# Five own buffers for the modulation columns in the SwiGLU stages, and a new division of the columns over the stages

## The chip, the cores and the metric

The kernel runs on one core of a Trainium2 chip. The metric is the time of one execution on the device in microseconds, as the median of several runs. The engines of a core work side by side, each through its own instructions in order: TensorE (PE; its weight loads stand apart as PEld), VectorE (DVE), ScalarE (ACT), GpSimd (POOL) and SyncE (SP), which here issues all loads.

## The reference, cut to what matters

A stream `x` of 256 tokens by 1024 channels goes through four layers. Each layer is a half-weighted SwiGLU part, a token mixer (RWKV-7, Mamba-2, sliding-window attention, RWKV-7) and a second SwiGLU part. Everything is float32. Ahead of each part the stream is normed and modulated by shift, scale and gate, which come from one vector `c`:

```python
c_act = jax.nn.silu(c)
...
    mod = (c_act @ ada_w[i] + ada_b[i]).reshape(bsz, N_SUB, 3, d)
    shift, scale, gate = mod[:, :, 0], mod[:, :, 1], mod[:, :, 2]
    h = adaln(x, norm_g[i, 0], shift[:, 0], scale[:, 0])
    x = x + MACARON_W * gate[:, 0, None] * swiglu(h, ffn_w_in[i, 0], ffn_w_out[i, 0])
...
def swiglu(h, w_in, w_out):
    a, b = jnp.split(h @ w_in, 2, axis=-1)
    return (jax.nn.silu(a) * b) @ w_out
```

`ada_w` has 1024 x 9216 numbers for each of the four layers, so 9 x 8 = 72 columns of 128 results, 288 in all. They depend on `c` alone: each can be computed at any time before the part that uses it.

## The kernel before

The stream stays in SBUF as `x`, eight tiles of 128 channels by 256 tokens. The stages follow each other: for layer i, `ffn{i}0`, the mixer, `ffn{i}2`, so eight SwiGLU stages (the text names them `ffn00` to `ffn32`, layer first) and four mixers: rw0 (RWKV), the Mamba stage, the attention stage and rw1 (the second RWKV stage, in layer 3).

**Units.** Weights come in units of 128 x 1024 numbers (512 KB). `unit` loads one into a `raw` buffer (four of them, pool `wp`), ScalarE copies it rounded to `whi` (L299), VectorE subtracts to get the rest, `wlo` (L303), and TensorE multiplies three times (L328 to L330, or L520 to L522 in the output projection): high by high, high by low, low by high. In a SwiGLU stage there are 66 units, 24 matmuls each: 44 into the two halves of the hidden part, 22 out of it. `weights` sets how many pairs `whi`, `wlo` are there: seven in a SwiGLU stage. The hidden tiles pass through `done` in `ffn` (L675 to L679). The output projection (`out_proj`) keeps sums of all eight tiles in PSUM and holds its last units back; when they come, each tile is summed into x (L608), and the next stage's operands are made of it at once (L491, L605).

**Columns.** One modulation column is one load of 512 KB and one operation on VectorE that multiplies, sums and adds the bias (L253; a readout of the sum belongs to it), and for scale and gate one more small operation (L257, L261). `mod_step` does both, and takes its buffer from the same four `raw` as the weights. `todo` is the list of columns in the order of use. In SwiGLU and Mamba stages `mod_tick` is called once in each unit and issues a column whenever its credit has grown to one; `mod_plan` sets how many a stage does (`QUOTA`) and over how many units. In the RWKV stages `mod_some` issues them at places in the code, up to the count `ahead`. Whatever is then still missing, `mod_until` issues right before it is used, which is in `out_proj`, ahead of the sums into x.

**Order.** A scheduler places the instructions on each engine's queue from the program and its dependencies. SP's queue is in order: a load that waits for its buffer holds up the loads behind it. `hold` and `issue_after` forbid some instructions to stand ahead of a given one.

## Time and profile before

| | |
|---|---|
| median of 3 runs | 2522.41 us (2514.05 to 2526.98) |
| profiled execution | 2529.85 us, its span 2527.9 us |
| columns in the twelve stages, in their order | 40, 36, 28, 28, 7, 28, 28, 13, 24, 24, 32, 0 |
| mean granted clock of TensorE | 0.962 of full speed |

Rows of groups give the line, the engine, the operation, its tiles as out<-in, the count, the busy time, the mean of one in ns, and the idle time of the engine ahead of them with what ended most of it. Rows that begin with two times are a stretch of the span and its length, the busy time of each engine with its instructions, the clock, the share of the DMA engines and their rate. Rows of waits name who waited, for whom, how long in all, how often and the longest. Rows of the timeline begin with the start and the duration in us.

### The profile page before, as it was taken

The page shows a single profiled execution, that of the slowest core. Times are in us where ns is not written, and L with a number is a line of the kernel's source. Part 1 is how long each engine was busy: PE and PEld are TensorE (multiplying, and loading weights), DVE is VectorE, ACT ScalarE, POOL GpSimd, SP SyncE. Part 2 cuts the span into 40 slices and gives each one's busy share as a digit, 9 for nine tenths or more (in the row PEclk, how much of TensorE's full clock was granted, in tenths as well). Part 3 has the DMA queues.
Part 4 walks back from the last instruction along what each step waited for, and adds up shares of the span by engine and source line. Part 5 has one row for each costly group of instructions (what it writes and reads, how often), then busy time and mean ns, then how long its engine had stood idle before and what let it go on. Part 6 is the DMA issues. An engine that isn't in the chain of part 4 may idle for free.

```text
span 2527.9 us, 51852 instructions
## 1 busy us (share of the span) xinstructions
PE 2403.7 (95%) x20868; PEld 2247.2 (89%) x20868; DVE 1984.8 (79%) x4181; ACT 1262.2 (50%) x2261; POOL 8.1 (0%) x14
## 2 busy tenths in 40 slices
PE   6999999989999989999999999899999999998999
PEld 5998877789999988999999999799999977777999
DVE  7777687887788788988878878987788767867754
ACT  3445663254454466765445446554444465623543
POOL 0000000000000000000000000000000000000000
PEclk9999898699999999999999999989999999987999
DMA  8874224668858834455885884468758732255653
GB/s 304 288 262 167 92 94 158 234 202 291 274 196 287 285 128 135 152 178 198 302 282 188 294 286 166 151 213 293 257 180 299 263 119 72 81 174 195 211 189 117
DMA packets 145392, 521.98 MB, mean 206 GB/s; under 512 B 16128, under 2 KB 19456, under 8 KB 145024
## 3 DMA queue, kind: packets, MB, share of 16 engines
q1 hardware_dynamic: 145152, 518.67, 60.3%
q8 instruction: 164, 2.69, 0.4%
q14 instruction: 76, 0.62, 0.1%
HBM read 516.50 MB, written 2.10 MB: 205 GB/s over the span
## 4 chain that ended last, share of the span: by engine, by line
PE 52%; DMA 20%; DVE 18%; ACT 5%; issue 5%; DVEq 0%; ACTq 0%; SPq 0%
DMA raw<-ffn 11%; PE aux L1077 8%; DMA ada<-ada_w 7%; DVE wlo L303 7%; PE aux L330 5%; PE aux L328 5%; PE aux L329 5%; PE mm L328 5%; PE mm L329 4%; PE mm L330 4%; PE mm L521 3%; DVE ada L253 3%; PE mm L520 3%; PE mm L522 3%; ACT whi L299 3%
## 5 line engine op out<-in xcount | busy, mean ns | idle before, releaser
L299 ACT CAST whi<-raw 128x1024 fp32r<-128x1024 f32 x671 | 699.9, 1049 | 696.1 <-DMA raw<-ffn 476.6
L303 DVE TENSOR_TENSOR wlo<-raw,whi 128x1024 fp32r<-128x1024 f32 x671 | 816.0, 1221 | 244.0 <-ACT whi L299 240.8
L328 PE MATMUL aux<-hh,whi 128*128 128x256 f32 x2576 | 723.7, 281 | 18.6 <-DVE ft L676 16.0
L330 PE MATMUL aux<-hh,wlo 128*128 128x256 f32 x2576 | 722.1, 281 | 12.7 <-DVE wlo L303 12.4
L329 PE MATMUL aux<-hl,whi 128*128 128x256 f32 x2576 | 720.3, 280 | 0.0
L328 PEld LDWEIGHTS aux<-hh,whi 128*128 128x128 f32 x2576 | 487.7, 189 | 24.7 <-DVE ft L676 20.1
L330 PEld LDWEIGHTS aux<-hh,wlo 128*128 128x128 f32 x2576 | 488.0, 190 | 16.1 <-DVE wlo L303 16.1
L329 PEld LDWEIGHTS aux<-hl,whi 128*128 128x128 f32 x2576 | 488.2, 190 | 0.0
L253 DVE CUSTOM_DVE_ANT_0 ada<-ada,cb,vec 128x1024 f32<-128x1024 f32 x288 | 368.3, 1280 | 82.9 <-DMA ada<-ada_w 82.2
L520 PE MATMUL mm<-gh,whi 128*128 128x256 f32 x1408 | 393.4, 281 | 9.9 <-ACT gh L678 9.9
L522 PE MATMUL mm<-gh,wlo 128*128 128x256 f32 x1408 | 391.7, 281 | 3.6 <-DVE wlo L303 3.5
L521 PE MATMUL mm<-gl,whi 128*128 128x256 f32 x1408 | 393.5, 281 | 0.8 <-DVE gl L679 0.5
L328 PE MATMUL mm<-hh,whi 128*128 128x256 f32 (+1 forms) x1056 | 311.3, 301 | 13.5 <-ACT cy L885 5.1
L329 PE MATMUL mm<-hl,whi 128*128 128x256 f32 (+1 forms) x1056 | 306.3, 293 | 0.4
L330 PE MATMUL mm<-hh,wlo 128*128 128x256 f32 (+1 forms) x1056 | 305.6, 292 | 0.0
L520 PEld LDWEIGHTS mm<-gh,whi 128*128 128x128 f32 x1408 | 266.9, 190 | 11.5 <-ACT gh L678 11.5
L522 PEld LDWEIGHTS mm<-gh,wlo 128*128 128x128 f32 x1408 | 266.2, 190 | 4.9 <-DVE wlo L303 4.8
L521 PEld LDWEIGHTS mm<-gl,whi 128*128 128x128 f32 x1408 | 267.0, 190 | 2.4 <-DVE gl L679 2.4
L328 PEld LDWEIGHTS mm<-hh,whi 128*128 128x128 f32 x1056 | 203.2, 195 | 27.7 <-issue 6.8
L329 PEld LDWEIGHTS mm<-hl,whi 128*128 128x128 f32 x1056 | 205.8, 195 | 8.7 <-issue 2.3
L330 PEld LDWEIGHTS mm<-hh,wlo 128*128 128x128 f32 x1056 | 205.3, 195 | 5.9 <-issue 4.3
L678 ACT ACTIVATE gh<-ft 128x256 fp32r<-128x256 f32 x176 | 73.0, 416 | 142.2 <-DVE ft L677 141.4
(357 smaller groups left out, 2998.7 us busy)
## 6 DMA issues: line engine op xcount, KB each, us to landing
raw<-ffn SPq DMA_DIRECT2D x522, 512.0 KB, 4.6
ada<-ada_w SPq DMA_DIRECT2D x288, 512.0 KB, 4.4
raw<-rkv SPq DMA_DIRECT2D x48, 512.0 KB, 3.3
raw<-mbin SPq DMA_DIRECT2D x48, 512.0 KB, 3.3
raw<-rwo SPq DMA_DIRECT2D x16, 512.0 KB, 4.6
raw<-mbout SPq DMA_DIRECT2D x16, 512.0 KB, 3.2
lora<-lora SPq DMA_DIRECT2D x12, 512.0 KB, 3.3
raw<-qkv SPq DMA_DIRECT2D x12, 512.0 KB, 4.0
```

Of the source, the lines that this page charges most:

```text
L253: nc.vector.tensor_tensor_reduce(out=raw, in0=raw, in1=self.cb, scale=1.0, scalar=self.v("ada_b", i * 72 + col), op0=ALU.mult, op1=ALU.add ...
L299: nc.scalar.copy(hi[:, :n], raw[:, :n])
L303: nc.vector.tensor_tensor(lo[:, :n], raw[:, :n], hi[:, :n].bitcast(F32), ALU.subtract)
L328: mm(out, hi, xh, start=start, stop=False)
L329: mm(out, hi, xl, start=False, stop=False)
L330: mm(out, lo, xh, start=False, stop=stop)
L520: mm(o, hi, xh, start=k == 0 and j % 2 == 0, stop=False, skip_group_check=True)
L521: mm(o, hi, xl, start=False, stop=False, skip_group_check=True)
L522: mm(o, lo, xh, start=False, stop=k == n - 1 and j % 2 == 1, skip_group_check=True)
L678: nc.scalar.activation(gh, t, AF.Copy, scale=0.5)
L1077: ins = nc.tensor.matmul(*a, **k)
```

## The change

In the SwiGLU stages the columns get a pool of their own, `ap`, of five buffers, and the pairs of prepared weights go from seven to six. A column is now fetched (`mod_fetch`) some time before it is computed: up to five are in hand (two in the first stage), one fetch in each unit. The computing begins ten units into the stage (in the first one at once) and is spread over 50 units instead of 52.8. The computation stands no longer in the scope of `hold`, but is bound to come after the subtraction of its unit (`part`). What is in hand at the end of a stage's hidden units is computed there.

The columns of the twelve stages become 40, 24, 33, 33, 6, 34, 34, 4, 32, 32, 8, 8. The attention stage has no rate of its own in either kernel: what it computes is what `mod_until` finds missing there. In rw0 four of the 24 are such, while none was before.

```diff
@@ -22,7 +22,7 @@
 S = 256
 DEPTH = 4
 
-QUOTA = ((24, 28), (28, 28), (28, 24), (24, 0))
+QUOTA = ((24, 33), (33, 34), (34, 32), (32, 8))
 DFF = 2816
 NJ = D // P
 NF = DFF // P
@@ -231,6 +231,7 @@
                     self.todo += [(i, s, 1, j), (i, s, 0, j)]
                 self.todo += [(i, s, 2, j) for j in range(NJ)]
         self.todo.reverse()
+        self.coming, self.apool, self.lead = [], None, 0
         self.credit = self.rate = 0.0
         self.st = None
         self.ready = []
@@ -244,12 +245,18 @@
         at, _ = V_AT[name]
         return self.vec[:, at + j : at + j + n]
 
+    def mod_fetch(self, pool, tag):
+        i, s, kind, j = self.todo.pop()
+        raw = pool.tile([P, D], F32, tag=tag, name="ada")
+        self.nc.sync.dma_start(raw, self.d["ada_w"][i, s * 24 + kind * 8 + j])
+        self.coming.append((raw, (i, s, kind, j)))
+
     def mod_step(self):
         nc = self.nc
-        i, s, kind, j = self.todo.pop()
+        if not self.coming:
+            self.mod_fetch(self.wp, "raw")
+        raw, (i, s, kind, j) = self.coming.pop(0)
         col = s * 24 + kind * 8 + j
-        raw = self.wp.tile([P, D], F32, tag="raw", name="ada")
-        nc.sync.dma_start(raw, self.d["ada_w"][i, col])
         nc.vector.tensor_tensor_reduce(
             out=raw, in0=raw, in1=self.cb, scale=1.0, scalar=self.v("ada_b", i * 72 + col),
             op0=ALU.mult, op1=ALU.add, accum_out=self.mod[i][:, s, kind, j : j + 1])
@@ -267,15 +274,18 @@
             self.mod_step()
 
     def mod_due(self, i, s, kind):
-        if not self.todo:
+        if not self.coming and not self.todo:
             return False
-        a = self.todo[-1]
+        a = self.coming[0][1] if self.coming else self.todo[-1]
         return (a[0], a[1], 2 if a[2] == 2 else 1) <= (i, s, kind)
 
-    def mod_plan(self, quota, units):
+    def mod_plan(self, quota, units, wait=0, pool=None, lead=0):
+
 
         self.quota = quota
-        self.rate, self.credit = quota / units, 0.0
+        self.rate = quota / units
+        self.credit = -wait * self.rate
+        self.apool, self.lead = pool, lead
 
     def mod_some(self, n, upto):
         while n and self.todo and len(self.todo) > 72 * DEPTH - upto:
@@ -284,9 +294,13 @@
 
     def mod_tick(self):
         self.credit += self.rate
-        while self.credit >= 1 and self.todo and self.quota:
+        if self.rate and self.apool and self.quota and self.todo and len(self.coming) < self.lead:
+            self.quota -= 1
+            self.mod_fetch(self.apool, "ada")
+        while self.credit >= 1 and (self.coming or self.todo and self.quota and not self.apool):
             self.credit -= 1
-            self.quota -= 1
+            if not self.coming:
+                self.quota -= 1
             self.mod_step()
 
 
@@ -300,7 +314,8 @@
         with ExitStack() as c:
             if self.hold is not None:
                 c.enter_context(self.tc.issue_after(self.hold))
-            nc.vector.tensor_tensor(lo[:, :n], raw[:, :n], hi[:, :n].bitcast(F32), ALU.subtract)
+            part = nc.vector.tensor_tensor(lo[:, :n], raw[:, :n], hi[:, :n].bitcast(F32), ALU.subtract).ins
+        with self.tc.issue_after(part):
             self.mod_tick()
         return hi, lo
 
@@ -651,13 +666,15 @@
         nc = self.nc
         self.phase(f"ffn{i}{s}")
         with ExitStack() as ctx:
-            self.weights(ctx, 7)
-            self.mod_plan(QUOTA[i][s // 2], 0.8 * 3 * NF)
+            self.weights(ctx, 6)
             gp1 = ctx.enter_context(self.tc.tile_pool(name="gp1", bufs=1))
             self.pad(gp1, "gp1", 192)
             pair = None if (i, s) == (0, 0) else self.pair(gp1)
             gp = ctx.enter_context(self.tc.tile_pool(name="gp", bufs=5))
             self.pad(gp, "gp", 0 if pair is None else 320)
+            ap = ctx.enter_context(self.tc.tile_pool(name="ap", bufs=5))
+            first = (i, s) == (0, 0)
+            self.mod_plan(QUOTA[i][s // 2], 50, 0 if first else 10, ap, 2 if first else 5)
             half = s // 2
             feed = self.out_proj(i, s, [self.d["ffn2"][i, half, f] for f in range(NF)])
             held, late = {}, []
@@ -686,6 +703,8 @@
                 self.dense_first(srcs, gp1, done, "aux")
             else:
                 self.dense_normed(i, s, srcs, gp1, done, tag="aux", pair=pair)
+            while self.coming:
+                self.mod_step()
             for g in late:
                 feed(*g)
             self.rate = 0.0
@@ -868,7 +887,7 @@
                 v.memset(t[:, 0:3], 0.0)
             tri2 = self.c("tri")[:, None, :].to_broadcast([P, 2, P])
 
-            self.mod_plan(8, 48)
+            self.mod_plan(6, 48)
             for g in range(8):
                 chans, zs = [], []
 
@@ -1071,7 +1090,7 @@
         self.phase(f"rw{i}")
         v, act = nc.vector, nc.scalar
         hold = [False]
-        ahead = 84 if i == 0 else 72 * DEPTH
+        ahead = 64 if i == 0 else 280
 
         def mm(*a, **k):
             ins = nc.tensor.matmul(*a, **k)
@@ -1453,7 +1472,8 @@
                     mm(o, flat(mid)[0:32, j * P : j * P + P], hm[0:32], start=False, stop=True)
                     v.tensor_tensor(y, y, o, ALU.mult)
                     self.split(oh[:, jj], ol[:, jj], y)
-                    self.mod_some(2, ahead)
+                    if jj % 2:
+                        self.mod_some(1, ahead)
                     feed(oh[:, jj], ol[:, jj])
                     yield 1
 
@@ -1577,7 +1597,7 @@
             yss[1] = slot("f1", [4, S], "ys")
             for jj in range(4):
                 read_heads(1, jj)
-                self.mod_some(2, ahead)
+                self.mod_some(1, ahead)
                 self.fill(3)
             hold[0] = False
             for _ in outputs(0, yt, g2, mid):
```

SP's queue in the middle of the second SwiGLU stage (ffn02); a number in a name grows with the place in the program. Before:

```order
L296 DMA raw_6254<-ffn1 128x1024
L252 DMA ada_6260<-ada_w 128x1024
L296 DMA raw_6295<-ffn2 128x1024
L296 DMA raw_6326<-ffn1 128x1024
L252 DMA ada_6332<-ada_w 128x1024
L296 DMA raw_6361<-ffn1 128x1024
L296 DMA raw_6399<-ffn2 128x1024
L252 DMA ada_6405<-ada_w 128x1024
```

After:

```order
L310 DMA raw_6280<-ffn1 128x1024
L310 DMA raw_6313<-ffn1 128x1024
L310 DMA raw_6355<-ffn2 128x1024
L251 DMA ada_6253<-ada_w 128x1024
L310 DMA raw_6388<-ffn1 128x1024
L310 DMA raw_6421<-ffn1 128x1024
L251 DMA ada_6319<-ada_w 128x1024
L310 DMA raw_6463<-ffn2 128x1024
L251 DMA ada_6361<-ada_w 128x1024
```

Before, a column's load stands among the weights in the program's order, and every load takes the next `raw` buffer. After, `ada_6253` stands behind `raw_6355`, which comes three units later in the program, and takes a buffer of its own pool.

VectorE's queue at the end of the attention stage, from before the first sum into x. Before:

```order
L257 SCALAR_TENSOR_TENSOR mod2_96<-mod2_96,vec_80 128x1
L608 SCALAR_TENSOR_TENSOR x_82<-mm_19886,mod2_96,x_82 128x256
L253 ISA ada_20336,mod2_96<-ada_20336,cb_83,vec_80 128x1024
L253 ISA mod2_96 128x1
L253 ISA ada_20340,mod2_96<-ada_20340,cb_83,vec_80 128x1024
L253 ISA mod2_96 128x1
L257 SCALAR_TENSOR_TENSOR mod2_96<-mod2_96,vec_80 128x1
L491 SCALAR_TENSOR_TENSOR hl_20358<-x_82,mod2_96,hh_20357 128x256
L253 ISA ada_20343,mod2_96<-ada_20343,cb_83,vec_80 128x1024
L253 ISA mod2_96 128x1
L608 SCALAR_TENSOR_TENSOR x_82<-mm_19887,mod2_96,x_82 128x256
```

After:

```order
L334 TENSOR_TENSOR ol_19069<-aux_20324,oh_19068 128x256
L264 SCALAR_TENSOR_TENSOR mod2_96<-mod2_96,vec_80 128x1
L260 ISA ada_20374,mod2_96<-ada_20374,cb_83,vec_80 128x1024
L260 ISA mod2_96 128x1
L623 SCALAR_TENSOR_TENSOR x_82<-mm_19937,mod2_96,x_82 128x256
L498 CAST hh_20377<-mod2_96 128x8x2
L623 SCALAR_TENSOR_TENSOR x_82<-mm_19938,mod2_96,x_82 128x256
```

Before, seven columns stand ahead of the first sum into x and six more among the next ones; after, four stand ahead of it and none behind.

VectorE's queue at the end of rw0, up to the second sum or up to what stands ahead of it. Before:

```order
L1454 TENSOR_TENSOR ys_5096<-ys_5096,aux_5415 128x256
L303 TENSOR_TENSOR wlo_5431<-raw_5428,whi_5430 128x1024
L319 TENSOR_TENSOR o_5335<-ys_5096,o_5334 128x256
L303 TENSOR_TENSOR wlo_5605<-raw_5602,whi_5604 128x1024
L303 TENSOR_TENSOR wlo_5611<-raw_5608,whi_5610 128x1024
L608 SCALAR_TENSOR_TENSOR x_82<-mm_5225,mod0_94,x_82 128x256
L608 SCALAR_TENSOR_TENSOR x_82<-mm_5226,mod0_94,x_82 128x256
```

After:

```order
L260 ISA ada_5558,mod0_94<-ada_5558,cb_83,vec_80 128x1024
L260 ISA mod0_94 128x1
L317 TENSOR_TENSOR wlo_5549<-raw_5546,whi_5548 128x1024
L264 SCALAR_TENSOR_TENSOR mod0_94<-mod0_94,vec_80 128x1
L260 ISA ada_5562,mod0_94<-ada_5562,cb_83,vec_80 128x1024
L260 ISA mod0_94 128x1
L623 SCALAR_TENSOR_TENSOR x_82<-mm_5208,mod0_94,x_82 128x256
L317 TENSOR_TENSOR wlo_5555<-raw_5552,whi_5554 128x1024
L260 ISA ada_5565,mod0_94<-ada_5565,cb_83,vec_80 128x1024
L260 ISA mod0_94 128x1
L260 ISA ada_5569,mod0_94<-ada_5569,cb_83,vec_80 128x1024
```

Before, the sums into x follow the last subtractions of weights directly; after, two of the four missing columns stand ahead of the first sum and two between it and the second.

## The prediction

> **What bounds the kernel now.** I read the page first, then the stages one by one, then what each engine waits for in a stage, and last the timeline where a wait is long.
>
> ```profile
> span 2527.9 us, 51852 instructions
> PE 2403.7 (95%) x20868; PEld 2247.2 (89%) x20868; DVE 1984.8 (79%) x4181; ACT 1262.2 (50%) x2261; POOL 8.1 (0%) x14
> L253 DVE CUSTOM_DVE_ANT_0 ada<-ada,cb,vec 128x1024 f32<-128x1024 f32 x288 | 368.3, 1280 | 82.9 <-DMA ada<-ada_w 82.2
> ada<-ada_w SPq DMA_DIRECT2D x288, 512.0 KB, 4.4
> ```
>
> TensorE is busy for 95% of the span, so at most 124 us of idle time can go, besides what a higher clock would give. The third row is the work that the change moves: 288 modulation columns of 1.28 us on VectorE, for which VectorE stood idle 82 us in all; each needs 512 KB. The stages, cut at the last matmul of each (length, busy TensorE, weight loads, VectorE, ScalarE and GpSimd, then clock, DMA share and GB/s):
>
> ```profile
> 228.60:509.50 280.90, 269.44 (x2736) 218.84 (x2735) 214.03 (x541) 136.69 (x294) 3.96 (x5) 0.87 0.41 141
> 509.50:710.00 200.50, 189.26 (x1594) 186.71 (x1595) 162.83 (x290) 98.35 (x151) 0.00 (x0) 0.98 0.75 251
> 710.00:904.70 194.70, 189.96 (x1594) 188.03 (x1593) 157.65 (x279) 94.92 (x143) 0.00 (x0) 0.99 0.74 252
> 1155.10:1348.00 192.90, 187.60 (x1595) 184.91 (x1594) 158.47 (x281) 95.98 (x144) 0.00 (x0) 1.00 0.76 257
> 1348.00:1540.80 192.80, 186.82 (x1594) 184.28 (x1594) 157.73 (x279) 94.41 (x142) 0.00 (x0) 1.00 0.77 257
> 1651.40:1844.50 193.10, 190.50 (x1595) 189.90 (x1594) 152.63 (x268) 95.06 (x143) 0.00 (x0) 0.99 0.72 246
> 1844.50:2043.60 199.10, 189.47 (x1594) 187.12 (x1593) 153.32 (x265) 94.66 (x142) 0.00 (x0) 0.97 0.71 241
> 2043.60:2333.10 289.50, 273.52 (x2769) 216.19 (x2768) 218.00 (x557) 139.13 (x297) 3.97 (x5) 0.90 0.38 130
> 2333.10:2524.60 191.50, 189.86 (x1593) 189.08 (x1591) 120.92 (x197) 89.71 (x132) 0.00 (x0) 0.99 0.50 170
> ```
>
> The first and the eighth row are the RWKV stages rw0 and rw1, the others SwiGLU stages. The last of these (ffn32) computes no column and takes 191.5 us with 1.6 us of idle TensorE: that is what a SwiGLU stage takes when weights are never late. The six others with columns are over it by 9.0, 3.2, 1.4, 1.3, 1.6 and 7.6 us, 24.1 in all. In ffn10 (third row) these waits stand ahead of that:
>
> ```profile
> ACT whi L299 <- DMA raw<-ffn: 61.6, 37, 5.0
> DVE wlo L303 <- ACT whi L299: 23.1, 20, 3.4
> DVE ada L253 <- DMA ada<-ada_w: 8.6, 9, 2.0
> ```
>
> ScalarE waits for weights, VectorE for ScalarE, and VectorE for columns: a ring of four `raw` buffers carries both. VectorE's 157.65 us of work and its 31.7 us of these waits fill 189.4 of 194.7 us. So the SwiGLU stages are at TensorE's pace with little slack in front of it.
>
> **The change part by part.** One column costs VectorE 1.28 us, its readout 0.08 and for two kinds of three a small operation of 0.15, so 1.46 us:
>
> ```profile
> L253 DVE CUSTOM_DVE_ANT_0 ada<-ada,cb,vec x288: 1262/1279/1289, 11.3 to 2303.1; 128x1024 f32<-128x1024 f32 x144
> L253 DVE DVE_READ_ACCUMULATOR2_ANT mod<- x288: 70/82/88, 12.5 to 2304.3; 128x1 f32 x144
> L257 DVE SCALAR_TENSOR_TENSOR mod<-mod,vec x96: 140/152/161, 12.8 to 2281.7; 128x1 f32<-128x1 f32 x96
> ```
>
> *SwiGLU stages.* The columns get five buffers of their own and their loads go out some units ahead. What this can take away is the 24.1 us above ffn32. I take two thirds, **-16 us**: the rest lies at the stages' starts, where sums and norms and not columns are late. Bounds: 0 (nothing gained, the pace is TensorE's) and -24. Five to eight more columns in a stage add up to 8 x 1.46 = 11.7 us on VectorE, in ffn32 as well. I cost them at nothing; the cover is the waits of VectorE just shown and, in ffn32, 70 us of idle VectorE. How dense the 50 counted units become is worked out from steady stretches of ffn10 and of ffn32:
>
> ```profile
> 740.00:900.00 160.00, 157.10 (x1326) 156.22 (x1327) 124.15 (x188) 73.22 (x98) 0.00 (x0) 0.99 0.82 279
> 2360.00:2520.00 160.00, 158.75 (x1348) 158.55 (x1348) 92.98 (x119) 69.33 (x93) 0.00 (x0) 1.00 0.53 180
> ```
>
> Without columns 1348 matmuls, 24 a unit, make 56.2 units in 160 us: 2.85 us a unit, in which VectorE works 1.655 us. With 33 columns in 50 units come 0.66 x 1.46 = 0.96 us: 2.62 of 2.85 us, 92%. Loads become 1.66 x 524,288 bytes in 2.85 us, 305 GB/s. Before, 28 columns in 52.8 units asked for 281, which is the first row's 279: that rate was the demand, at a share of 0.82, so a full share would be about 340. The highest stretch that I find is where columns alone are loaded, at the end of the attention stage:
>
> ```profile
> 1640.00:1650.00 10.00, 5.06 (x22) 4.76 (x23) 10.00 (x28) 2.57 (x7) 0.00 (x0) 0.50 0.92 319
> ```
>
> So 305 GB/s fits, at a share of about 0.9. Here the Trainium skill, in "DMA: Bandwidth & Descriptors" (section Bandwidth), speaks against the change: it wants 1 MiB or more in a transfer for three quarters of the peak, and its section on the anatomy of a DMA gives about 2 us fixed plus the bytes at 436 GB/s, by which 512 KB take about 3.2 us (an estimate from that page). By that, 83 transfers one after another would take 266 us. The trace does not agree: at 279 GB/s one transfer takes 1.88 us, as several are in flight. The same page puts the limit of HBM for one core at about 358 GB/s, and by this 305 fits too.
>
> SP issues in order, and a column's load waits for VectorE to free its buffer, with weights queued behind it. In the order, that load stands some three weight loads later than its place in the program, and the column whose buffer it takes is freed about when the next weight's buffer is, so I cost it at nothing; if VectorE is late, up to one column (1.46 us) is added to a weight's load, which up to six prepared weight pairs cover.
>
> *Six pairs of prepared weights for seven.* In the first stage the six hold the opening weights until their last matmul; the seventh unit then waits for a cast and a subtraction. Their durations are in the rows of whi (1049 ns) and wlo (1221 ns):
>
> ```profile
> L299 ACT CAST whi<-raw 128x1024 fp32r<-128x1024 f32 x671 | 699.9, 1049 | 696.1 <-DMA raw<-ffn 476.6
> L303 DVE TENSOR_TENSOR wlo<-raw,whi 128x1024 fp32r<-128x1024 f32 x671 | 816.0, 1221 | 244.0 <-ACT whi L299 240.8
> ```
>
> That is **+2 us**, from -4 (the freer ring makes up for it) to +4. Elsewhere one pair less is 2.85 us less in front; I cost it at nothing, since four `raw` buffers for weights alone stand behind it.
>
> *Attention stage.* Thirteen columns were computed in one go at its end, ahead of the sums into x:
>
> ```profile
> 1626.23 1.28 DVE L253 CUSTOM_DVE_ANT_0 ada<-ada,cb,vec 128x1024 f32<-128x1024 f32 x1
> 1627.43 0.42 DVE L319 TENSOR_TENSOR ol<-aux,oh 128x256 fp32r<-128x256 f32 x1
> 1627.77 0.55 DVE L803 COPY pt<-aux 128x384 f32<-128x384 f32 x1
> ...
> 1636.38 0.48 DVE L608 SCALAR_TENSOR_TENSOR x<-mm,mod,x 128x256 f32<-128x256 f32 x1
> 1636.91 0.58 PE L520 MATMUL mm<-oh,whi 128*128 128x256 f32 x1 [4.60 <-DVE x L608]
> 1642.35 0.58 PE L520 MATMUL mm<-oh,whi 128*128 128x256 f32 x1 [3.15 <-DVE x L608]
> 1647.23 0.58 PE L520 MATMUL mm<-oh,whi 128*128 128x256 f32 x1 [2.59 <-DVE x L608]
> ```
>
> TensorE waited 10.3 us for three sums. Now four columns are left, all ahead of the first sum. They take 4 x 1.46 = 5.8 us and three other operations that stand between them about 1.4 (0.42 twice and 0.55); the thirteen began at 1626.2, so the four end near 1633, where TensorE began to wait (1636.91 - 4.60 = 1632.31). The first wait shrinks to about 1 us and the others go: **-9.5 us**, bounds -6 (loads late) and -12 (9 x 1.46 = 13, a little of it hidden).
>
> *RWKV stages.* rw1 computes 8 columns instead of 32, the eight in its chain; rw0 24 instead of 36. In rw1's closing part a short iteration on VectorE had a column between its steps:
>
> ```profile
> 2267.67 0.17 DVE L1168 TENSOR_SCALAR m<-mm 128x16 f32<-128x16 f32 x1
> 2304.55 0.38 PE L1081 MATMUL aux<-con,ry 128*8 128x128 f32 x2 [2.61 <-DVE ry L593]
> 2277.00:2333.10 56.10, 49.27 (x245) 38.87 (x246) 43.17 (x102) 17.05 (x28) 0.00 (x0) 0.72 0.61 207
> ```
>
> The first norm was begun at 2267.67, and the second was still awaited at 2304.55. TensorE was idle 6.8 of the last 56.1 us. 24 columns are 35 us of VectorE, but most of TensorE's work there goes on beside them. I take that idle time as the term, **-7 us**; bounds 0 and -16, the stage's whole idle time (289.50 - 273.52). What is late next is TensorE's own output products. In rw0 twelve columns go (17.5 us of VectorE, TensorE idle 11.5 us in the stage), but four to five now stand at its end, three of them ahead of the first sum into x, behind which the next stage's start is queued: 5 x 1.46 = 7.3 us at worst, if nothing covers them. I take **-3 us**, from +7 to -11. The Mamba stage computes 6 for 7 columns, **-1** (0 to -1.5).
>
> **Sum:** -16 + 2 - 9.5 - 7 - 3 - 1 = -34.5 us. The profiled execution took 2529.85 us, 1.95 more than its span, so its like would take 2495.4. The three runs shown have the median 2522.41, 7.4 less; from there the sum gives 2487.9, and **2488 us** is the forecast. All best bounds (-24, -4, -12, -16, -11, -1.5) give 2454, all worst (0, +4, -6, 0, +7, 0) give 2527.
>
> **Rivals.** *The clock follows.* In the closing parts of rw0 and rw1 TensorE ran at half clock while its records fill the time:
>
> ```profile
> 455.00:470.00 15.00, 15.00 (x44) 10.51 (x44) 14.37 (x31) 3.31 (x5) 0.00 (x0) 0.50 0.72 246
> 485.00:500.00 15.00, 15.00 (x51) 11.23 (x50) 10.91 (x26) 2.93 (x5) 0.00 (x0) 0.52 0.60 195
> 2275.00:2290.00 15.00, 12.74 (x42) 8.54 (x42) 13.83 (x38) 4.97 (x8) 0.00 (x0) 0.59 0.84 271
> 2305.00:2320.00 15.00, 14.17 (x38) 9.45 (x39) 9.15 (x19) 3.44 (x7) 0.00 (x0) 0.50 0.42 148
> ```
>
> If products that no longer wait for VectorE keep the clock at 1.0 there, 15 x (0.50 + 0.48 + 0.41 + 0.50) = 28 us could go at most; half of it is 14, and the time 2474. For it: a column no longer breaks the row of products. Against it: 14.17 of 15 us counted as busy and the clock was still 0.50. The rule "TensorE: Matmul & The Clock Gate" of the Trainium skill (Part 1) would side with it: there the clock doubles after a window of about 3.4 us of busy TensorE. The four rows do not agree with it as they stand, unless busy by the records is not busy for the gate.
>
> *VectorE takes the place of the loads.* At 2.62 of 2.85 us a unit there is 0.23 us of slack. If its waits for ScalarE stay (23.1 us in 66 units, 0.35 a unit), a unit takes 2.97 us, and 50 units are 6 us longer; in six stages 36 us, which eats the sum: 2524. For it: VectorE is in order, and a late cast holds up everything. Against: those casts were late because weights shared their ring with columns.
>
> *The loads saturate* (slower). If 280 GB/s, the most that stood for 160 us, is what one queue can hold, the 83 transfers of 50 counted units (43.5 MB) take 155 us instead of 142.5 at TensorE's pace: 13 us in each of six stages, 77 in all, against 20.5 gained outside them and 2 lost: 2522 + 59 = 2581. It decides where the sustained rate stays under 305 GB/s. Against it stand the 319 GB/s and that 281 was only the demand.
>
> **How the numbers follow.** The forecast has 0.70 (0.64 of it faster by over 0.5%, the rest within), the clock 0.15, VectorE 0.08, saturated loads 0.07. 0.5%, or 12.6 us, is about what a measurement of this kernel tells from no change. So faster 0.79, within 0.14, slower 0.07. The range reaches from 2450, past the best bounds and the clock's half, to 2512; above it are left saturated loads, VectorE's case and the worst corner of the bounds.
>
> **What would show it.** Right: the six SwiGLU stages at 191 to 195 us; no wait of columns for their DMA there; a DMA share of 0.8 and more for those stages; the three waits for x at the attention stage's end down to one of about 1 us; rw1's closing without the wait for L593. Wrong: SwiGLU stages above 195 us with VectorE waiting for casts (second rival), or with the time of a load to landing well above 4.4 us and ScalarE waiting for weights (third); a wait of several us for x at rw0's end would cancel its term.

## The result, and the profile after

The changed kernel took **2427.14 us** (median of four runs, 2421.40 to 2435.14), the kernel before 2523.19 (four runs). The ratio is **0.9638, 95% interval 0.9609 to 0.9667**; the medians are 96 us apart, where 34.5 were forecast, and the time lies below the range of the prediction. The profiled execution took 2425.33 us, its span 2423.5.

The rows of the page of the changed kernel that answer to those of before (the groups with count, busy time, mean ns of one, idle time ahead):

```profile
span 2423.5 us, 51913 instructions
PE 2352.3 (97%) x20868; PEld 2207.8 (91%) x20868; DVE 1976.8 (82%) x4181; ACT 1264.1 (52%) x2261; POOL 8.1 (0%) x14
L260 DVE CUSTOM_DVE_ANT_0 ada<-ada,cb,vec 128x1024 f32<-128x1024 f32 x288 | 367.8, 1278 | 4.7 <-DMA ada<-ada_w 4.7
ada<-ada_w SPq DMA_DIRECT2D x288, 512.0 KB, 5.3
```

The wait of columns for their loads, 82.9 us before, is 4.7. Busy TensorE fell by 51.4 us (2403.7 before) with the same 20868 matmuls: half of the 104 us between the two profiled spans stands in the records as busy time, as matmuls that follow each other more closely. The stages (length, busy TensorE, weight loads, VectorE, ScalarE, GpSimd, clock, DMA share, GB/s), rw0 first, rw1 last but one:

```profile
221.70:499.50 277.80, 263.23 (x2737) 212.34 (x2735) 201.20 (x510) 137.73 (x296) 3.97 (x5) 0.89 0.35 120
499.50:685.30 185.80, 183.38 (x1594) 183.21 (x1595) 164.97 (x304) 98.41 (x147) 0.00 (x0) 0.99 0.83 298
685.30:868.20 182.90, 182.49 (x1594) 181.71 (x1593) 164.54 (x290) 94.48 (x142) 0.00 (x0) 1.00 0.77 269
1121.90:1305.30 183.40, 182.60 (x1594) 181.79 (x1593) 163.87 (x300) 95.83 (x144) 0.00 (x0) 1.00 0.84 302
1305.30:1487.60 182.30, 181.94 (x1594) 181.55 (x1594) 163.03 (x293) 96.01 (x143) 0.00 (x0) 1.00 0.78 275
1584.10:1767.50 183.40, 182.64 (x1594) 181.86 (x1594) 162.11 (x296) 95.74 (x145) 0.00 (x0) 1.00 0.83 296
1767.50:1950.10 182.60, 182.33 (x1593) 181.73 (x1593) 161.94 (x286) 95.26 (x142) 0.00 (x0) 1.00 0.77 271
1950.10:2236.70 286.60, 276.47 (x2770) 221.02 (x2769) 189.07 (x489) 139.07 (x297) 3.97 (x5) 0.88 0.25 87
2236.70:2420.30 183.60, 182.70 (x1592) 181.87 (x1591) 130.35 (x222) 89.71 (x133) 0.00 (x0) 1.00 0.59 200
```

Each of the seven later SwiGLU stages is under the 191.5 us that the prediction took as its floor. ffn32, which had no columns before and now computes eight, is 7.9 us shorter.

**Two rhythms.** In the middle of these stages TensorE counts as busy all the time, and still does more or fewer matmuls. Three stretches of the changed kernel, of ffn10, ffn32 and ffn00; the prediction shows ffn32 of before, 1348 matmuls in 160 us:

```profile
700.00:860.00 160.00, 159.69 (x1405) 159.30 (x1403) 145.03 (x234) 79.91 (x113) 0.00 (x0) 1.00 0.85 295
2255.00:2415.00 160.00, 159.22 (x1402) 159.01 (x1401) 109.90 (x167) 77.64 (x111) 0.00 (x0) 1.00 0.57 192
60.00:220.00 160.00, 160.00 (x1361) 160.00 (x1360) 124.89 (x187) 75.67 (x104) 0.00 (x0) 1.00 0.76 268
```

One matmul follows the other after 113.3 ns or after 117.8 ns (113.33 and 117.78 as means of steady stretches, taken from the starts of successive matmuls in the trace), at the same granted clock of 1.00. The recorded expectations below say 117.5 and a difference of 4.2; it is 4.4. One of the two holds for up to 1400 matmuls in a row. In the two profiles of the kernel before, all 35 changes from one steady stretch to the other (12 matmuls or more each) stand behind an interval above 0.16 us; 59 more such breaks changed nothing. In the first 20 us of a stage, where the intervals scatter, a steady row also begins without one. Over about 1500 matmuls of a SwiGLU stage the slow rhythm costs 4.4 ns x 1500 = 6.6 us. Below, **stops** are the intervals above 0.16 us between the starts of two matmuls, less 0.113 us each: idle TensorE in whatever rhythm.

| first profile of each | six stages, sum | stops: first sixth, middle, last sixth | slow matmuls in all eight |
|---|---|---|---|
| before | 1173 us | 31.9, 23.3, 11.9 | 6058 |
| after | 1100 us | 8.6, 0.0, 2.3 | 2104 |

The six stages are ffn02 to ffn30. They lost 56 us of stops; the rest of their 73 us is mostly the rhythm, some 3400 matmuls fewer in the slow one (15 us). Outside the SwiGLU stages, attention went from 110.6 to 96.5 us, rw0 and rw1 by 3 us each, and Mamba rose by 3.

### The profile page after: what moved, and what is told of

Its sections match the earlier page's. It is cut to its first block, busy times and chain, and to the rows that moved or that the text cites. A ratio compares the mean times of both kernels' runs of the same rounds, so it can differ in the third digit from the quotient of the medians.

```text
span 2423.5 us, 51913 instructions
## 1 busy us (share of the span) xinstructions
PE 2352.3 (97%) x20868; PEld 2207.8 (91%) x20868; DVE 1976.8 (82%) x4181; ACT 1264.1 (52%) x2261; POOL 8.1 (0%) x14
## 4 chain that ended last, share of the span: by engine, by line
PE 86%; DVE 8%; ACT 3%; DMA 2%; issue 1%; SPq 0%; DVEq 0%; ACTq 0%
PE aux L345 12%; PE aux L343 12%; PE aux L344 12%; PE aux L1096 9%; PE mm L535 7%; PE mm L536 7%; PE mm L537 7%; PE mm L343 5%; PE mm L344 5%; PE mm L345 5%; DVE wlo L317 2%; PE mm L1096 2%; DMA raw<-ffn 1%; DVE ada L260 1%; ACT whi L313 1%
## 5 line engine op out<-in xcount | busy, mean ns | idle before, releaser
L345 PE MATMUL aux<-hh,wlo 128*128 128x256 f32 x2576 | 713.8, 277 | 0.5 <-DVE wlo L317 0.4
L343 PE MATMUL aux<-hh,whi 128*128 128x256 f32 x2576 | 713.7, 277 | 0.0
L535 PE MATMUL mm<-gh,whi 128*128 128x256 f32 x1408 | 388.4, 277 | 3.1 <-ACT gh L695 3.1
```

The lines of the kernel that those rows point to most:

```text
L343: mm(out, hi, xh, start=start, stop=False)
L345: mm(out, lo, xh, start=False, stop=stop)
L535: mm(o, hi, xh, start=k == 0 and j % 2 == 0, stop=False, skip_group_check=True)
```

## The experiments

Each ratio is to the kernel before, run beside it on the same chip, with its 95% interval. The stage sums are those of the table above, from the one profile of each kernel. Theory: the time comes from stops, which three parts of the change remove together (the own buffers with their early loads, the ten units of waiting, and the tie, that is, a column's computation bound behind the subtraction of its unit), and from the rhythm. Rivals: the new division of the columns; the own buffers alone; the rhythm as a property of the new order.

| kernel | ratio | six stages | stops: start, middle, end | attention | rw1 |
|---|---|---|---|---|---|
| before, second profile | | 1168 | 31.6, 20.3, 4.5 | 110.4 | 295.5 |
| after_again | 0.9648 (0.9579 to 0.9717) | 1107 | 10.6, 0.0, 1.1 | 96.3 | 276.0 |
| no_columns | 0.9480 (0.9426 to 0.9534) | 1103 | 8.1, 0.0, 0.1 | 95.0 | 277.2 |
| pool_only | 1.0069 (1.0036 to 1.0103) | 1190 | 52.9, 1.8, 43.5 | 109.9 | 296.9 |
| new_division | 1.0117 (1.0060 to 1.0174) | 1217 | 36.1, 44.0, 33.6 | 96.3 | 274.1 |
| old_tie | 0.9966 (0.9937 to 0.9994) | 1191 | 45.2, 3.1, 34.2 | 96.1 | 281.1 |
| untied | 0.9954 (0.9916 to 0.9992) | 1192 | 47.0, 6.7, 42.3 | 96.3 | 283.0 |
| no_wait | 0.9829 (0.9779 to 0.9879) | 1155 | 34.6, 9.5, 7.3 | 96.7 | 273.8 |
| no_pool | 1.0078 (1.0050 to 1.0105) | 1213 | 9.3, 24.4, 75.9 | 96.2 | 272.5 |
| old_division | 0.9746 (0.9706 to 0.9786) | 1106 | 8.4, 0.0, 0.5 | 110.1 | 299.0 |
| six_pairs | 1.0113 (1.0076 to 1.0149) | 1185 | 29.5, 18.3, 31.5 | 114.8 | 288.8 |
| seven_three | 0.9637 (0.9593 to 0.9681) | 1122 | 8.1, 1.3, 9.5 | 96.1 | 270.8 |
| two_edits | 0.9625 (0.9589 to 0.9661) | 1105 | 8.8, 0.0, 1.4 | 96.8 | 277.9 |
| one_break | 0.9658 (0.9620 to 0.9697) | 1112 | 9.4, 0.0, 1.9 | 96.4 | 276.1 |

### What is the floor, and what is the rhythm?

**after_again** is the changed kernel itself, and **before_again** the kernel before.

> The changed kernel once more, for a second profile. In both profiles so far TensorE's matmuls in a SwiGLU stage start either 113.3 ns or 117.5 ns after one another, for hundreds of matmuls in a row, and a change of this rhythm comes only after a stop of TensorE. In the first profile of the changed kernel ffn00 was in the slow rhythm and the seven others in the fast one. Theory A (the rhythm is set by the kernel's order and layout): the same eight rhythms again, each SwiGLU stage within 0.5 us of the first profile (ffn00 221.7, the others 182.4 to 185.8). Theory B (it is chance at each start): at least one of the eight stages changes its rhythm, and is 6 to 7 us longer or shorter than in the first profile (1590 x 4.2 ns). Time about 2427 by both.

> The kernel before once more, for a second profile. The prediction took ffn32 without columns, 191.5 us, as what a SwiGLU stage takes. If the slow rhythm that ffn32 was in is chance at each start, the rhythms of several stages are others in this profile, stage by stage with stops of the same sums (ffn32 about 4 us, ffn02 16, ffn30 17), and ffn32 takes either 185 or 191.5 us; if the order sets it, the lengths of all eight stages are within 1 us of the first profile. Time 2505 to 2530.

ffn12 and ffn32 of the changed kernel, 183.4 and 183.6 us in its first profile, in the second:

```profile
1128.10:1316.80 188.70, 188.27 (x1595) 187.85 (x1594) 164.35 (x300) 96.32 (x145) 0.00 (x0) 1.00 0.83 293
2238.70:2428.40 189.70, 188.76 (x1593) 187.91 (x1592) 130.55 (x222) 89.77 (x133) 0.00 (x0) 1.00 0.57 194
```

And ffn32 of the kernel before, 191.5 us in its first profile, in its second:

```profile
2332.00:2517.10 185.10, 183.38 (x1592) 182.59 (x1591) 120.58 (x197) 89.37 (x132) 0.00 (x0) 0.99 0.52 176
```

Theory B holds: the same kernel, the same stage, the same work, 6 us apart with the same small idle time. The order doesn't fix the rhythm of these stages (ffn00 alone was in the slow one in both). The 191.5 us were a stage in the slow rhythm, and the next profile of the same kernel had it in the fast one.

**no_columns** computes none of the columns and fills shift, scale and gate with 0.1:

```diff
-        i, s, kind, j = self.todo.pop()
+        if not self.todo:
+            return
+        i, s, kind, j = self.todo.pop()
...
-        self.todo.reverse()
+        self.todo = []
+        for m in self.mod:
+            self.nc.vector.memset(m, 0.1)
```

> The kernel before with no modulation column computed at all: shift, scale and gate are set to 0.1 and no ada_w is loaded. It asks what a SwiGLU stage takes when nothing shares the ring with its weights. By the prediction's floor each of the seven later SwiGLU stages takes 191.5 us, as ffn32 did. By the rhythm theory they take 183 to 186 us in the fast rhythm and 190 to 192 in the slow one, and at least one of the seven is in the fast one; stops of TensorE sum to under 4.1 us in each. Time by the floor about 2460, by the rhythm theory 2410 to 2455.

Its ffn10 and ffn22:

```profile
648.20:830.30 182.10, 181.99 (x1595) 181.60 (x1594) 123.37 (x204) 94.06 (x141) 0.00 (x0) 1.00 0.56 189
1542.50:1731.30 188.80, 188.44 (x1594) 187.84 (x1594) 124.59 (x207) 96.10 (x146) 0.00 (x0) 1.00 0.55 185
```

The true floor is **182 us** in the fast rhythm and 189 in the slow one, with VectorE a third idle. The median was 2387.1 us, under the 2410 expected: rw0 without its 36 columns took 257.4 us instead of 280.9, and its clock was 0.95 instead of 0.87. At an equal rhythm the stages ffn02 to ffn30 of the changed kernel's first profile are at most 1.3 us longer than those of a kernel that computes no columns at all.

**breaks** puts a small product into the row after every sixth hidden tile:

```diff
             def done(q, out):
+                if q % 6 == 1:
+                    t = self.bank("aux", 2)
+                    nc.tensor.matmul(t[:, 0:1], self.ones, self.ones[:, 0:1], start=True, stop=True)
```

> The changed kernel with a small extra product of one column (128x1, into a spare buffer of PSUM that nothing reads) after every sixth tile of a SwiGLU stage's hidden part, eight in a stage. It asks whether a break in the row of equal matmuls sets the rhythm anew. If any break does, the rows of equal rhythm end at the extra products, and within single stages both rhythms stand, ffn00 among them, which was in the slow one throughout in six profiles of its order; stages of 184 to 189 us. If only a stop for data does, the rhythm of a stage goes on across the extra products as it was. Time 2425 to 2450.

Four stretches of its ffn12, each between two such products:

```profile
1166.00:1189.00 23.00, 23.00 (x205) 23.00 (x205) 21.51 (x35) 11.94 (x18) 0.00 (x0) 1.00 0.81 288
1191.00:1214.00 23.00, 23.00 (x198) 23.00 (x197) 19.71 (x32) 9.90 (x13) 0.00 (x0) 1.00 0.88 314
1217.00:1240.00 23.00, 23.00 (x205) 23.00 (x204) 21.66 (x35) 11.37 (x15) 0.00 (x0) 1.00 0.98 360
1242.00:1265.00 23.00, 23.00 (x198) 23.00 (x197) 18.47 (x29) 10.27 (x14) 0.00 (x0) 1.00 0.92 320
```

205 and 198 matmuls in turn: the break turned the rhythm over, from fast to slow behind all 24 products that met the fast one, from slow to fast behind 30 of the 39 that met the slow one. So this break sets it, and not by a throw of the dice alone. The one run took 2461.25 us, more than expected; half of all matmuls were in the slow rhythm. **one_break** tried to use the break: one product in ffn00 alone (and the four early columns of two_edits, below).

> The changed kernel with the four early columns in rw0 of the run with two edits, and one extra product of one column (128x1) in the first stage, after its eighth hidden tile, near 109 us of the span. If a fixed break turns the rhythm over (in the run with eight breaks a stage the rhythm was the other one behind nearly every break, and behind this one in the first stage the fast one), ffn00 goes on in the fast rhythm from there: 217 to 218 us instead of 221.6, with the same 22 us of stops; rw0 275 us with about 2 us of waits for x at its end instead of 7.6. Time 2412 to 2424. If the break gives chance alone, ffn00 stays at 221.6 in about half of the cases; time 2420 to 2432.

Median 2429.28 us. The scheduler placed the product at 54.8 us of the span, not at 109, where the row was in the fast rhythm for the moment; behind it the slow one held to the stage's end (ffn00 221.7 us). This shows nothing of the product: without it the same row went from fast to slow at 60.5 us in after_again and at 54.8 us in two_edits. How to choose the fast rhythm stays open.

### Which part removes the stops?

**pool_only** is the kernel before with buffers, early fetch and six pairs, shown here as an edit of the changed kernel (the mixers have their old numbers too); **new_division** is the kernel before with nothing but the new QUOTA and the new numbers in the mixers.

```diff
-QUOTA = ((24, 33), (33, 34), (34, 32), (32, 8))
+QUOTA = ((24, 28), (28, 28), (28, 24), (24, 0))
...
-        with self.tc.issue_after(part):
             self.mod_tick()
...
-            self.mod_plan(QUOTA[i][s // 2], 50, 0 if first else 10, ap, 2 if first else 5)
+            self.mod_plan(QUOTA[i][s // 2], 0.8 * 3 * NF, 0, ap, 2 if first else 5)
```

> The kernel before with the five own buffers, the early fetch and six pairs, but the old division of columns (28, 28, 28, 28, 24, 24, 0 in the later SwiGLU stages, 36, 7, 13, 32 in the mixers), the old 52.8 units and the column in the old place, within the hold and not tied to its unit. Theory 1 (own buffers take away the stops of TensorE): the six later SwiGLU stages with columns go to 183 to 188 us, attention stays at about 110 and rw1 at about 290; time 2455 to 2465. Theory 2 (the buffers gain nothing without the tie or the new division): those stages stay at 190 to 200 and the time at 2510 to 2530.

> The kernel before with only the new division of columns over the stages: more columns in SwiGLU stages (33, 33, 34, 34, 32, 32, 8), fewer in the mixers, all still through the four raw buffers, seven pairs of prepared weights. Theory 1 (the stops come from the shared ring): attention is 10 to 14 us shorter, rw0 and rw1 3 us each, but the SwiGLU stages gain nothing or lose 1 to 3 us each; time 2500 to 2530. Theory 2 (the gain comes from the division): time at 2460 or lower.

Neither gains: 2536.20 and 2548.72 us. The theory that the own buffers alone take the stops away fell: with six pairs they cleared the middle of the stages (1.8 us left of 23.3), and the starts and ends became worse. The division shortens attention as expected and rw1 by more than the 3 us expected, and costs the six SwiGLU stages with their shared ring 44 us, where 1 to 3 us a stage were expected. Four kernels leave one part out of the changed kernel. **old_tie** computes the column within the hold, unbound:

```diff
-        with self.tc.issue_after(part):
             self.mod_tick()
```

> The changed kernel, but a unit's column computation stands within the hold again and isn't bound behind the subtraction of its unit; buffers, six pairs, the ten units of waiting and the new division stay. Theory C (own buffers clear the middle of a stage, the tie clears its end, the ten units clear its start): the ends of ffn02, ffn12 and ffn22 get stops of TensorE again, 13 to 16 us each as in the run with the buffers alone, the starts and the middles stay free of them; time 2460 to 2475. Rival D (the waiting clears both): no stage more than 3 us longer than in the changed kernel beyond the 6 to 7 us of a changed rhythm; time 2425 to 2435.

**no_wait** begins the columns with the stage's first unit:

```diff
-            self.mod_plan(QUOTA[i][s // 2], 50, 0 if first else 10, ap, 2 if first else 5)
+            self.mod_plan(QUOTA[i][s // 2], 50, 0, ap, 2 if first else 5)
```

> The changed kernel, but the computing of columns begins with a stage's first unit instead of ten units later, at the same rate of 50 units. Theory C: the stops in the first sixth of a SwiGLU stage, 0.1 to 3 us in the changed kernel, rise to 5 to 11 us in the six stages with 32 to 34 columns as in the run with the buffers alone; ends and middles stay free; time 2455 to 2475. Rival E (the tie alone clears the starts as well): stops there stay under 3 us, time 2425 to 2435.

**no_pool** fetches a column when it is computed, into a `raw` buffer:

```diff
-            ap = ctx.enter_context(self.tc.tile_pool(name="ap", bufs=5))
...
-            self.mod_plan(QUOTA[i][s // 2], 50, 0 if first else 10, ap, 2 if first else 5)
+            self.mod_plan(QUOTA[i][s // 2], 50, 0 if first else 10)
```

> The changed kernel without the pool: each column is fetched when it is computed and takes one of the four raw buffers; tie, waiting, division and six pairs stay. Theory C: stops in the middle of the SwiGLU stages come back, 5 to 13 us a stage as in the run with the new division alone, starts and ends stay clear; time 2470 to 2520. Rival F (the order on VectorE's queue is all of it, buffers nothing): SwiGLU stages at 182 to 190, time 2425 to 2440.

**old_division** has the old QUOTA and the old numbers in the mixers, undoing those lines of the diff:

```diff
-QUOTA = ((24, 33), (33, 34), (34, 32), (32, 8))
+QUOTA = ((24, 28), (28, 28), (28, 24), (24, 0))
```

> The changed kernel with the division of columns of before (28, 28, 28, 28, 24, 24, 0 in the later SwiGLU stages, 36, 7, 13, 32 in the mixers). Theory C (the division matters for the mixers alone): SwiGLU stages as in the changed kernel, attention at 110 instead of 96, rw1 up to 10 us longer; time 2440 to 2455. Rival G (the stages' stops come back without the new division): time above 2460.

Against the changed kernel's 2427.1 us: without the tie 2507.5 (+80), without the ten units 2476.0 (+49), without the pool 2536.2 (+109), with the old division 2452.6 (+25). Theory C had the starts right for no_wait (34.6 us of stops for 8.6), with a time 1 us above its range; but it put the middles and ends at nothing, and they had 9.5 and 7.3. It had the time right for old_division, where rw1 became 12 to 23 us longer and not up to 10. For the two others it was too low: the tie matters at the starts too (45.2 us of stops), and without the pool it is the ends that suffer most (75.9). The division matters for the mixers alone, as expected. The four losses sum to 264 us, far over the 96 gained: the parts of the order are not a sum. Without the pool nothing is left of the gain, and without the tie less than half a per cent of the time; without the ten units half of it is left.

Why the tie matters, **untied** shows. Out of the hold, but not bound:

```diff
-        with self.tc.issue_after(part):
-            self.mod_tick()
+        self.mod_tick()
```

> The changed kernel with a column's computation outside the hold but not bound behind the subtraction of its unit: of the two halves of the tie only the first. If the hold was what sent columns and weights ahead of the hidden tiles at the stage ends (the run with the old tie was 80 us longer), this kernel is as the changed one, 2420 to 2440. If the binding is needed, the stops at the ends of ffn02, ffn12 and ffn22 are there again, 8 to 15 us each, and at the starts 4 to 9; time above 2470.

The median was 2507.51 us: the binding does it. The column operations of VectorE alone (two instructions a column) in ffn12 and ffn20, of the changed kernel:

```profile
1121.90:1305.30 183.40, 43.72 (x68) 1.00 0.84 302
1305.30:1487.60 182.30, 43.76 (x68) 1.00 0.78 275
```

And of untied:

```profile
1152.10:1361.50 209.40, 61.78 (x96) 0.95 0.83 299
1361.50:1551.60 190.10, 25.68 (x40) 0.98 0.64 225
```

The program asks for 34 and 34 columns. Unbound, 48 and 20 are computed: 14 of ffn20's columns stand in VectorE's queue ahead of ffn12's end. The timeline of VectorE there, and what TensorE waited for in the last 30 us of untied's ffn12 (its lines are one less than the changed kernel's):

```profile
1336.34 1.28 DVE L260 CUSTOM_DVE_ANT_0 ada<-ada,cb,vec 128x1024 f32<-128x1024 f32 x1 [2.53 <-DMA ada<-ada_w]
...
1346.41 1.28 DVE L260 CUSTOM_DVE_ANT_0 ada<-ada,cb,vec 128x1024 f32<-128x1024 f32 x1
1347.61 0.08 DVE L260 DVE_READ_ACCUMULATOR2_ANT mod<- 128x1 f32 x1
1347.61 0.42 DVE L692 SCALAR_TENSOR_TENSOR ft<-ft,aux 128x256 f32<-128x256 f32 x1
1347.95 1.28 DVE L260 CUSTOM_DVE_ANT_0 ada<-ada,cb,vec 128x1024 f32<-128x1024 f32 x1
```

```profile
PE mm L534 <- ACT gh L694: 9.8, 2, 7.4
ACT whi L313 <- DMA raw<-ffn: 8.2, 4, 4.1
```

Columns that nobody needs yet stand between the steps of the last hidden tiles (`ft` at L692, then `gh`), one of them waiting 2.53 us for its load, and TensorE waits 9.8 us for `gh`. The same waits in the changed kernel's last 30 us:

```profile
PE mm L535 <- ACT gh L695: 0.3, 1, 0.3
ACT whi L313 <- DMA raw<-ffn: 4.0, 3, 2.4
```

ScalarE's wait for weights doubled as well, from 4.0 to 8.2 us. How much of the 9.8 us is the columns' place on VectorE's queue, and how much the weights that came late beside their loads, isn't separated.

Unbound, ffn02, ffn12 and ffn22 had the stops at their ends: they are the stages that another SwiGLU stage follows directly, whose columns could run ahead. In no_pool no column ran ahead (34 and 34), and the ends of the stages suffered from the shared ring: in the last 30 us of its ffn12 ScalarE waited for weights, and TensorE for `gh` behind that:

```profile
ACT whi L313 <- DMA raw<-ffn: 8.8, 5, 2.3
...
PE mm L535 <- ACT gh L694: 8.0, 2, 7.2
```

### Six pairs, the first stage, rw0

**six_pairs** sets `weights(ctx, 6)` in the kernel before; **seven_three** sets it to 7 in the changed kernel, with three column buffers and three fetched ahead. **two_edits** has, in the changed kernel:

```diff
             for j in range(4):
                 bonus(j)
+                if i == 0:
+                    self.mod_some(1, ahead)
...
-            self.mod_plan(QUOTA[i][s // 2], 50, 0 if first else 10, ap, 2 if first else 5)
+            self.mod_plan(QUOTA[i][s // 2], 50, 10, ap, 5)
```

> The kernel before with six instead of seven pairs of prepared weights in the SwiGLU stages, nothing else. The prediction's term: the first stage 2 us longer (-4 to +4), the other stages within the 7 us of a changed rhythm; time 2510 to 2530. Rival (the seventh pair is what covers the columns' share of the ring): stops of TensorE in the SwiGLU stages rise by 5 us or more each; time above 2545.

> The changed kernel with seven pairs of prepared weights again and three column buffers, three fetched ahead (two in the first stage as now), in about the same SBUF. If six pairs are enough and five buffers are what matters: stops come back in the SwiGLU stages, 2 us or more each, time above 2440. If three buffers are enough: stops stay at 1 to 3 us a stage and the first stage loses 0 to 4 of its 22 us of stops; time 2415 to 2435.

> The changed kernel with two edits in stages that don't touch each other, each read from its own stage. In rw0 four more columns are placed ahead of the chain, beside the bonus terms, so that none is missing at its end: the waits of TensorE for x there, 7.6 us in the changed kernel, go back to about 4 as with the old division; rw0 2 to 6 us shorter at an equal clock. In ffn00 the computing of columns begins ten units in as in the other stages, with five fetched ahead. If the columns cause its 22 us of stops in the first quarter, these fall to the 17 us of the kernel without columns, ffn00 5 us shorter; if the weights alone cause them, nothing there changes but the rhythm, which was the slow one in all five profiles of that same ffn00 order: if the order decides it, it may change for good, 6 us less. Time 2405 to 2425.

six_pairs took 2545.57 us, 26.7 more than the kernel before beside it: 2.6 in the first stage, as the prediction had it, and 6 to 7 us of stops at the ends of ffn10, ffn12, ffn20 and ffn30 (of which before had only ffn30's, in one profile of two). The time is the rival's by half a microsecond; its 5 us a stage were not reached everywhere. seven_three took 2430.58, as the changed kernel, with 7.3 us of stops at ffn02's end: in the new order a seventh pair in exchange for buffers four and five is worth nothing that can be measured. What each is worth by itself there wasn't run.

two_edits took 2427.71. ffn00 kept its 22.4 us of stops and its slow rhythm, so the computing of the 24 columns, which was put off, doesn't cause them. Without any column ffn00 had 17.0; what makes the other 5 stays open, since the loads of the columns, and the 16 other columns of that stage, were not put off. rw0's end, in the kernel before, in the changed kernel, and then in two_edits:

```profile
PE mm L328 <- DVE x L608: 2.5, 1, 2.5
PE mm L520 <- DVE x L608: 1.4, 1, 1.4
```

```profile
PE mm L535 <- DVE x L623: 6.3, 2, 4.9
PE mm L343 <- DVE x L623: 1.3, 1, 1.3
```

```profile
PE mm L535 <- DVE x L623: 1.9, 1, 1.9
```

The waits for x shrank by 5.7 us and rw0 took 275.2 us instead of 277.8 and 282.7; in the whole time that doesn't show. No version that computes all the columns beats the changed kernel.

## Why the prediction was wrong, point by point

- **The failed step is the floor.** "That is what a SwiGLU stage takes when weights are never late": ffn32's 191.5 us hold 6.6 us of slow rhythm (1511 matmuls x 4.4 ns) and 3.9 us of stops. Measured against it, ffn12 was 1.4 us over and seemed done; against the true 182 us it was 11 over, 9.0 of them stops. The "24.1 in all" and the bound of -24 followed from it. The six stages had 67 us of stops (56 in the second profile); 56 and 45 of them went. With two profiles of each kernel the six stages gave 1171 - 1104 = **67 us for the 16 forecast**.
- **The starts were left out for the wrong reason.** A third of the 24 us was taken as lost to the starts, "where sums and norms and not columns are late". The starts gave 23 of their 32 us of stops, and no_wait, which differs from the changed kernel only in beginning the columns with the first unit, had 34.6 again.
- **What told it was in the quoted rows.** 1348 matmuls in 158.75 busy us are 117.8 ns each, at a clock of 1.00; other stages of before had stretches at 113. Equal stretches of ffn20 and of ffn32, both without idle time:

```profile
1385.00:1405.00 20.00, 20.00 (x179) 20.00 (x178) 16.80 (x26) 9.11 (x12) 0.00 (x0) 1.00 0.90 295
2400.00:2420.00 20.00, 20.00 (x173) 20.00 (x171) 11.09 (x14) 8.83 (x12) 0.00 (x0) 1.00 0.57 187
```

  Busy TensorE was read as a limit, and its pace was not compared between stages.
- **The tie had no price.** The prediction cost the loads' order, and not that a column's computation could stand in a stage that doesn't ask for it. Leaving the tie out costs 80 us.
- **One pair less** was costed at 2 us in the first stage and "nothing" elsewhere. By itself it costs 26.7 us; behind the new order, in exchange for the two column buffers, nothing.
- **The first stage** was to lose 2 us and gained 7: its stops fell from 33.3 to 22.3.
- **Attention**: -9.5 forecast, -14.1 measured in both pairs of profiles. The wait for x fell from 10.3 to 0.5 us, as forecast; 4.2 us are busy time (95.96 to 91.74), at a clock of 0.86 before and 1.00 after in the closing 55 us. In the rows of before and of after, with the wait of after:

```profile
1596.10:1651.40 55.30, 41.42 (x318) 36.15 (x316) 52.48 (x172) 24.03 (x75) 0.00 (x0) 0.86 0.62 210
```

```profile
1528.80:1584.10 55.30, 50.82 (x427) 44.31 (x427) 51.66 (x231) 32.86 (x105) 0.00 (x0) 1.00 0.38 125
PE mm L535 <- DVE x L623: 0.5, 1, 0.5
```

- **rw1**: -7 forecast. The first pair of profiles shows -2.9, the second -19.5: the clock of this stage differs between executions (0.88 and 0.91 after). Over the five profiles with 32 columns there (288.8 to 299.0) and eleven with 8 (270.8 to 286.6) the means are 293.9 and 277.6: **-16, the best bound**. The closing 56.1 us took 372 matmuls for 245, at 0.82 for 0.72:

```profile
2180.60:2236.70 56.10, 54.03 (x372) 43.47 (x368) 28.95 (x77) 16.30 (x33) 0.00 (x0) 0.82 0.19 67
```

- **The rival that the clock follows** was half right at most. In the last sixth of rw1 the clock was 0.71 to 0.75 in all five profiles with 32 columns and 0.81 to 0.88 in all eleven with 8; in the closing 55 us of attention 0.85 to 0.88 in the same five and 1.00 in the same eleven. So it goes with the division. In rw0's closing part it did not follow (0.72 in the last sixth of both). And no_columns, with no column in either, had 0.76 in rw1's last sixth and 0.85 in rw0's: that the waits of the products for VectorE set the clock is not shown.
- **rw0**: -3 forecast, -3.1 and +6.3 in the two pairs. The wait feared at its end came (7.6 us for 3.9) and took back what the fewer columns gave. Mamba was 3 us longer and not 1 shorter; why stayed open.
- **VectorE in the loads' place** did not happen: it was busy 165 of 185.8 us in ffn02, and TensorE had no stops in the middle. **The loads did not saturate**: 302 GB/s stood for all of ffn12, where 305 had been worked out. Here the Trainium skill, in "DMA: Bandwidth & Descriptors", section Specifications, gives about 358 GB/s as one core's limit at HBM; the 360 GB/s of a stretch of 23 us in the run with breaks reach it, in transfers of 512 KB. The 2 us and 436 GB/s that the prediction took from that page are fitted there to transfers that GpSimd issues; here SP issues them.

So of the 96 us between the medians, the eight SwiGLU stages gave 76 (mean of two profiles each: 1588 and 1512), 63 of them stops and some 12 the rhythm; attention 14 and rw1 11 in the same profiles; rw0 and Mamba took back 5. That the change makes the fast rhythm likelier is not shown: slow matmuls were 51 and 52% before, 17 and 39% after.

## What to carry to other kernels

Take the floor of a stage from several stages or executions, and compare the matmuls in a stretch, not only its busy share: a busy engine can run at two paces. Work that is needed later must be bound to its place on an engine's queue as well as be given buffers; with buffers alone a scheduler moves it ahead, here into the end of an earlier stage, where TensorE waited for that very engine. Leave each part of a change out once: here the buffers without the bound place, and the bound place without the buffers, were worth next to nothing.

## What the runs showed of the hardware

TensorE has two steady rhythms for the same row of weight loads and 256-column products: 113.3 and 117.8 ns from start to start at a granted clock of 1.00 (276 and 281 ns by the records of one). The work of the other engines doesn't go with it: ffn10 and ffn22 of the kernel without columns have the same work and different rhythms. It changes behind breaks of the row: behind 54 of 63 products of one column in the run with breaks, and behind 35 of 94 stops between steady stretches in the two profiles of the kernel before. What it is inside TensorE no run here shows. The Trainium skill, "TensorE: Matmul & The Clock Gate" (Back-to-back issue gap), gives N / 2.4 + 2.5 ns for an isolated matmul on a warm array, which is an estimate of 109.2 ns for 256 columns, and for a sustained stream of weight loads and matmuls about 81 ns at 128 columns and 131 ns at 512, with none for 256. Both measured values are above the estimate, and that section names no second pace for the same stream.
